# Moving the additions of weight blocks in DRAM out of the up-projection and into the part before it

## The chip, the cores and the metric

The kernel runs on one core of a Trainium2 chip. The metric is the device time of one execution in microseconds (us); the kernel before takes 1739.53 us as the median of 3 runs (1737.74 to 1740.78). The engines are called as in the profile: PE (matrix products), PEld (its weight loads), DVE (vector), ACT (scalar), POOL (GpSimd, which here only issues DMAs that add into their destination), and SP, whose queue issues nearly all other DMAs.

## The reference, cut to what matters

One decoder block on 256 tokens of width 2048, all in float32:

```
u    = rmsnorm(x)
proj = u @ w_in                     # columns of HGRN (q, f, i, gate), of attention (q, k, v), of two merge gates
ya   = hgrn2(...) @ w_proj_a        # gated linear recurrence, 16 heads of 128
yb   = dilated_attention(...) @ w_proj_b
mix  = sigmoid(gate_a) * ya + sigmoid(gate_b) * yb
h    = x + mix @ w_out
v    = rmsnorm(h)
hup  = v @ w_up                     # 2048 x 11264
hc   = causal_conv3(hup) + conv_b   # per channel
h    = h + (gelu(hc[:, :5632]) * hc[:, 5632:]) @ w_down
out  = rmsnorm(h)
```

## The kernel before, in words

**Units.** All weights lie in DRAM in the order of their use, as 300 units of 1 MB (128 partitions x 16 blocks of 128). Units 0 to 35 are the attention's columns of `w_in`, 36 to 99 those of HGRN, 100 to 131 the two gates, 132 to 151 `w_proj_b` and `w_proj_a`, 152 to 167 `w_out`, 168 to 299 the up-projection `w_up` in 11 blocks with pieces of `w_down` between them. `load(u)` has SP fetch a unit into one of three `raw` buffers (L303; L297 and L298 for the units described next). Each float32 weight is then cut into a high part, made by ACT (`hl`, L380), and the rest, made by DVE (L381), since a product is made from three PE passes: low input x high weight, high x high, high x low (L537 to L539 and L598 to L600). A pair of such parts stays in one of four `pair` buffers (six in the up-projection) until PE has read it. `begin_unit(u)` splits up to two units ahead of PE and loads three ahead.

**Two ways through w_up.** 88 units belong to `w_up`. 28 of them are mode "P" and have plain products. 60 are mode "S": seven products in place of eight, in the manner of Strassen and Winograd. An S unit needs sums of its four 512-column blocks of weights. Two of these sums, q1 and q2, are made in DRAM long before the unit is loaded; the others are made on DVE (L354, L355). `load` then fetches three blocks of the unit (L297), q1 as the fourth (L298, `raw<-q`) and q2 into a buffer of its own (L300, `q<-q`; two such buffers).

**The additions in DRAM.** The function `add_blocks` makes one turn. A turn starts q1 for the next S unit: SP copies a weight block to a DRAM tile (`q<-weights`, L266) and POOL adds another block to it by a DMA that adds (L267). The same turn also finishes the q2 of the S unit three turns earlier: SP copies its q1 (`q<-q`, L266, shown with a shape of 16x4096) and POOL adds a third block (L267). SP's copies stand behind the last weight load issued so far (`in_turn(loaded[-1])`). POOL's additions stand in POOL's queue in the order of the turns and each waits for its copy to land; SP's copy of q1 waits until the addition to q1 has landed. There are 60 S units and 63 turns, hence 120 copies and 120 additions of 256 KB.

**When a turn is taken.** `begin_unit(u)` makes turns until their number is `additions(u)`. In the kernel before that is 51 turns spread evenly from unit 44 to unit 166, and after that one turn every 8 units, up to unit 262. This means that the last 12 turns are made while `w_up` is worked on.

**The other work of POOL and ACT in w_up.** After a block of `w_up` its 512 columns are unfolded from seven PSUM banks (`up0v`, `up0c` and so on, with the block's number), transposed on PE (`ua3t`, `ub3t`, L1028), convolved (ACT writes the taps `ua3e`, `ub3e` at L1036, DVE adds them at L1038) and gated. Between blocks PE makes partial sums of `w_down` (`dn`). ACT copies each from PSUM to a buffer `dns` (L1078) and POOL adds it to `h` by a DMA (`h<-dns`, L1079). The buffers of `dns`, of the taps and of the unfolding come from one ring of five (`stage`), so one that waits for its DMA holds up ACT's next write into the ring.

**What sets the order.** Each engine has one queue and works in its order. The order is made by a scheduler from the program text, from priorities and from estimated durations, so that the place of an instruction can move when another one is moved. The diff touches only constants and the function `additions`.

Of the kernel before, what the change touches and what calls it, by code (L numbers as in the profile page):

```python
# [130 lines left out]
MODES = stream_spec()[1]  # L131

DRAM_SUMS = sorted(u for u, mode in MODES.items() if mode == "S")
ADD_FROM, ADD_TO, ADD_LATE = 44, 166, 8


def additions(u):
    n = len(DRAM_SUMS) + 3
    if u <= ADD_TO:
        return max(0, (u - ADD_FROM) * (n - 12) // (ADD_TO - ADD_FROM))  # L140
    return min(n, n - 12 + (u - ADD_TO) // ADD_LATE)

# [49 lines left out]
def hybrid_block(ctx, tc, x_p, x_t, weights, g1, gf, params, c_rope, c_mask0, c_mask1, c_level, out):  # L194
# [219 lines left out]
    def begin_unit(u):  # L414
        for v in range(u, u + LOOKAHEAD + 1):
            split(v)
        load(u + LOOKAHEAD + 1)
        pump(SIDE_US)
        while added[0] < additions(u):
            add_blocks()  # L420
            added[0] += 1
# [742 lines left out]
```

## Time and profile before

| what | value |
|---|---|
| time of the profiled execution | 1738.46 us |
| its span, first to last instruction | 1736.7 us |
| median of the runs | 1739.53 us |
| PE busy | 1713.5 us, 99% |
| DVE, ACT, POOL busy | 75%, 61%, 8% |
| mean granted PE clock | 0.998 |
| 16 DMA engines, mean moved | 240 GB/s |

The page divides the span into shares of busy time; a view of stretches gives the busy time of each engine between two times and the share of the DMA engines' time. A matmul's busy time overlaps that of the next (one starts some 0.23 us after the other and is shown with 0.39 us), so that a short wait of PE hardly shows in its busy time. The list of PE's waits and the number of matmuls in a stretch show it better. By the times at which the products of a stage start, the stages lie so: HGRN's columns to 619 us, the gates 619 to 805, `w_proj_b` and `w_proj_a` 805 to 917, `w_out` 917 to 1008, `w_up` and `w_down` from 1008 on.

### The profile page before, as it was taken

Reading aid. Unit: us, or ns where it says so; the run is one execution under the profiler, and the core shown is the slowest. Engines: PE = TensorE matmul, PEld = TensorE weight load, DVE = VectorE, ACT = ScalarE, POOL = GpSimd, SP = SyncE. Lnnn points to the kernel's source line nnn. Section 1 sums busy time; section 2 is a strip of 40 time slices with the busy share of each in tenths; the row PEclk is TensorE's granted clock in tenths of the full one; section 3 lists DMA queues with packets and bytes.
Section 4 is the critical chain, followed back from the end, with each engine's and each line's share of the span. In section 5 each row is a group of like instructions: output and inputs, shape, how many; then the busy total and the mean of one; then the engine's idle time right before and its main releaser. Section 6 shows DMA issues by size and latency. Waiting matters only on the chain. (4 is left out here: it accounts for less than half of the span.)

```text
span 1736.7 us, 22219 instructions
## 1 busy us (share of the span) xinstructions
PE 1713.5 (99%) x8292; PEld 1428.7 (82%) x8292; DVE 1301.3 (75%) x1559; ACT 1053.7 (61%) x1436; POOL 140.5 (8%) x181
## 2 busy tenths in 40 slices
PE   9999999999999999999999999999999999999998
PEld 8888888888888888888888887787777878888886
DVE  7765575776858675444656688999889889889886
ACT  6444465555455554544445568877776777887773
POOL 0000000011111011011111100110110110110000
PEclk9999999999999999999999999999999999999999
DMA  7765634778778787889998977887787788787672
GB/s 279 232 207 201 232 145 160 229 230 242 229 247 243 225 257 224 259 271 289 293 272 249 274 231 249 277 254 249 210 286 258 229 279 269 217 263 262 204 263 97
DMA packets 98684, 416.19 MB, mean 240 GB/s; under 512 B 11936, under 2 KB 12192, under 8 KB 67152
## 3 DMA queue, kind: packets, MB, share of 16 engines
q1 hardware_dynamic: 73344, 365.22, 58.5%
q0 software_dynamic: 23936, 46.15, 16.3%
q10 hardware_dynamic: 1296, 3.41, 0.5%
q8 instruction: 65, 1.06, 0.2%
q14 instruction: 43, 0.35, 0.1%
HBM read 400.05 MB, written 65.01 MB: 268 GB/s over the span
## 5 line engine op out<-in xcount | busy, mean ns | idle before, releaser
L380 ACT ACTIVATE hl<-raw 128x1024 fp32r<-128x1024 f32 (+1 forms) x480 | 500.9, 1055 | 502.1 <-PE egp L539 79.1
L381 DVE TENSOR_TENSOR hl<-raw,hl 128x1024 fp32r<-128x1024 f32 (+1 forms) x480 | 579.2, 1218 | 292.2 <-ACT hl L380 290.5
L267 POOL DMA_DIRECT2D q<-weights x120 | 99.7, 901 | 1113.3 <-DMA q<-q 821.3
L537 PE MATMUL dn<-hl,ff 128*128 128x512 f32 x320 | 126.7, 399 | 0.2 <-DVE up2c L621 0.2
L539 PE MATMUL dn<-hl,ff 128*128 128x512 f32 x320 | 125.0, 391 | 0.0
L538 PE MATMUL dn<-hl,ff 128*128 128x512 f32 x320 | 124.7, 390 | 0.0
L537 PE MATMUL egp<-hl,xu 128*128 128x512 f32 x256 | 100.5, 393 | 0.0
L539 PE MATMUL egp<-hl,xu 128*128 128x512 f32 x256 | 99.8, 390 | 0.0
L538 PE MATMUL egp<-hl,xu 128*128 128x512 f32 x256 | 99.7, 389 | 0.0
L328 DVE TENSOR_TENSOR se<-raw,se 128x1024 fp32r<-128x1024 f32 x60 | 73.2, 1221 | 16.6 <-ACT se L327 16.5
L327 ACT ACTIVATE sf<-raw 128x1024 fp32r<-128x1024 f32 x60 | 64.0, 1067 | 30.7 <-DVE raw L355 30.2
L328 DVE TENSOR_TENSOR sa<-raw,sa 128x1024 fp32r<-128x1024 f32 x60 | 73.2, 1220 | 9.8 <-ACT sa L327 9.8
L328 DVE TENSOR_TENSOR sf<-raw,sf 128x1024 fp32r<-128x1024 f32 x60 | 73.3, 1222 | 8.4 <-ACT sf L327 8.2
L327 ACT ACTIVATE se<-raw 128x1024 fp32r<-128x1024 f32 x60 | 63.9, 1066 | 25.1 <-PE up L600 12.6
L539 PEld LDWEIGHTS dn<-hl,ff 128*128 128x128 f32 x320 | 60.1, 188 | 13.1
L537 PEld LDWEIGHTS dn<-hl,ff 128*128 128x128 f32 x320 | 60.1, 188 | 12.7 <-DVE up2c L621 0.6
L538 PEld LDWEIGHTS dn<-hl,ff 128*128 128x128 f32 x320 | 60.2, 188 | 11.6
L327 ACT ACTIVATE sa<-raw 128x1024 fp32r<-128x1024 f32 x60 | 63.7, 1061 | 8.6 <-PE dn L539 4.9
L450 PE MATMUL ak<-xu,hl 128*128 128x512 f32 x192 | 67.1, 394 | 0.0
L539 PEld LDWEIGHTS egp<-hl,xu 128*128 128x128 f32 x256 | 48.1, 188 | 9.9
L538 PEld LDWEIGHTS egp<-hl,xu 128*128 128x128 f32 x256 | 48.1, 188 | 9.7
L537 PEld LDWEIGHTS egp<-hl,xu 128*128 128x128 f32 x256 | 48.1, 188 | 9.7
(585 smaller groups left out, 4417.6 us busy)
## 6 DMA issues: line engine op xcount, KB each, us to landing
raw<-weights SPq DMA_DIRECT2D x238, 1024.0 KB, 5.4
raw<-weights SPq DMA_DIRECT2D x60, 768.0 KB, 5.8
q<-weights POOLq DMA_DIRECT2D x120, 256.0 KB, 7.4
q<-q SPq DMA_DIRECT2D x120, 256.0 KB, 5.1
q<-weights SPq DMA_DIRECT2D x60, 256.0 KB, 6.3
raw<-q SPq DMA_DIRECT2D x60, 256.0 KB, 6.1
h<-dns POOLq DMA_DIRECT2D x36, 256.0 KB, 6.2
h<-x_t ACTq DMA_DIRECT2D x4, 512.0 KB, 6.6
```

The lines of the kernel that those rows point to most:

```text
L267: nc.gpsimd.dma_start(q, weights[u, :, i * 512 : (i + 1) * 512], accum_op=ALU.add)
L327: act.activation(hi, src, AF.Copy)
L328: vec.tensor_tensor(lo, src, hi.bitcast(F32), op=ALU.subtract)
L380: last[0] = act.activation(hi[:, q * w : (q + 1) * w], raw, AF.Copy)
L381: last[1] = vec.tensor_tensor(lo[:, q * w : (q + 1) * w], raw, hi[:, q * w : (q + 1) * w].bitcast(F32), op=ALU.subtract)
L450: pe.matmul(ps, hi, pair, start=(k == 0), stop=False, skip_group_check=True)
L537: pe.matmul(pst[m], xl, hi, start=(k == k0), stop=False)
L538: pe.matmul(pst[m], xh, hi, start=False, stop=False)
L539: pe.matmul(pst[m], xh, lo, start=False, stop=(k == k0 + nk - 1))
```

## The change

`additions` gets other constants. The turns now run from unit 40: 49 of them up to unit 132, at 0.533 per unit where it was 0.418, and the remaining 14 up to unit 166, at 0.412 per unit. From unit 168 on, where `w_up` begins, there are none. The number of turns, copies and additions is the same, and so are their sizes and everything that is computed.

```
-ADD_FROM, ADD_TO, ADD_LATE = 44, 166, 8
+ADD_FROM, ADD_THEN, ADD_TO, THEN_ADDS = 40, 132, 166, 14


 def additions(u):
     n = len(DRAM_SUMS) + 3
-    if u <= ADD_TO:
-        return max(0, (u - ADD_FROM) * (n - 12) // (ADD_TO - ADD_FROM))
-    return min(n, n - 12 + (u - ADD_TO) // ADD_LATE)
+    if u <= ADD_THEN:
+        return max(0, (u - ADD_FROM) * (n - THEN_ADDS) // (ADD_THEN - ADD_FROM))
+    return min(n, n - THEN_ADDS + (u - ADD_THEN) * THEN_ADDS // (ADD_TO - ADD_THEN))
```

PE and DVE work in the same order as before. What moves are instructions of SP and POOL, and one of ACT. In the rows below a name is the tile, its number (a unit's, or for `dns` and `dn` a block's with the quarter of the output) and a number of the tile's instance.

POOL in the first blocks of `w_up`, before: additions for later units stand between the additions of `w_down`'s partial sums.

```order
L267 DMA q2_269_7843<-weights 128x512
L267 DMA q1_273_8659<-weights 128x512
L1079 DMA h0_7267<-dns1_0_0_8772 128x512
L1079 DMA h0_7267<-dns1_0_1_8775 128x512
L1079 DMA h1_7269<-dns1_1_0_8837 128x512
L1079 DMA h1_7269<-dns1_1_1_8840 128x512
L267 DMA q2_270_7913<-weights 128x512
L267 DMA q1_274_9066<-weights 128x512
L1079 DMA h2_7271<-dns2_2_0_9251 128x512
L1079 DMA h2_7271<-dns2_2_1_9254 128x512
```

The same place after the change: the last addition for a weight block stands ahead of the first partial sum.

```order
L267 DMA q2_285_7587<-weights 128x512
L267 DMA q2_286_7657<-weights 128x512
L1079 DMA h0_7339<-dns1_0_0_8820 128x512
L1079 DMA h0_7339<-dns1_0_1_8823 128x512
L1079 DMA h1_7341<-dns1_1_0_8885 128x512
L1079 DMA h1_7341<-dns1_1_1_8888 128x512
L1079 DMA h2_7343<-dns2_2_0_9293 128x512
L1079 DMA h2_7343<-dns2_2_1_9296 128x512
```

All 21 additions that POOL made among or just ahead of these partial sums have moved to the time before `w_up`.

SP in the gates, before: two or three weight loads between two turns.

```order
L303 DMA raw116_5771<-weights 128x2048
L303 DMA raw117_5812<-weights 128x2048
L266 DMA q2_221_5482<-q1_221_5481 16x4096
L266 DMA q1_225_5814<-weights 128x512
L303 DMA raw118_5850<-weights 128x2048
L303 DMA raw119_5887<-weights 128x2048
L266 DMA q2_222_5580<-q1_222_5579 16x4096
L266 DMA q1_226_5889<-weights 128x512
L303 DMA raw120_5925<-weights 128x2048
L303 DMA raw121_5957<-weights 128x2048
L303 DMA raw122_5989<-weights 128x2048
L266 DMA q2_224_5681<-q1_224_5680 16x4096
```

The same units after the change: two, and at times only one.

```order
L303 DMA raw116_5831<-weights 128x2048
L303 DMA raw117_5872<-weights 128x2048
L266 DMA q2_238_5590<-q1_238_5589 16x4096
L266 DMA q1_246_5874<-weights 128x512
L303 DMA raw118_5910<-weights 128x2048
L303 DMA raw119_5947<-weights 128x2048
L266 DMA q2_244_5689<-q1_244_5688 16x4096
L266 DMA q1_248_5949<-weights 128x512
L303 DMA raw120_5985<-weights 128x2048
L266 DMA q2_245_5796<-q1_245_5795 16x4096
L266 DMA q1_249_5987<-weights 128x512
L303 DMA raw121_6023<-weights 128x2048
```

On ACT one row moves, after the second block of `w_up`. Before, the copy of the first partial sum stood ahead of two splits:

```order
L616 ACTIVATE up1c12_8724<-up1v_8719,rstd2_r_8015 128x512
L1078 ACTIVATE dns1_0_0_8772<-dn1_0_1_8735 128x512
L380 ACTIVATE hl186_0_8737<-raw186_8692 128x1024
L380 ACTIVATE hl186_1_8740<-raw186_8692 128x1024
L327 ACTIVATE sa187_8783<-raw187_8743 128x1024
```

Now it stands behind them:

```order
L616 ACTIVATE up1c12_8772<-up1v_8767,rstd2_r_8075 128x512
L380 ACTIVATE hl186_0_8785<-raw186_8740 128x1024
L380 ACTIVATE hl186_1_8788<-raw186_8740 128x1024
L1078 ACTIVATE dns1_0_0_8820<-dn1_0_1_8783 128x512
L327 ACTIVATE sa187_8831<-raw187_8791 128x1024
```

## The prediction

> **What bounds the kernel now.** I read the page's busy times first, then the stretches by stage, then PE's waits, and last the landings of DMAs and POOL's queue around the longest wait.
>
> ```profile
> PE 1713.5 (99%) x8292; PEld 1428.7 (82%) x8292; DVE 1301.3 (75%) x1559; ACT 1053.7 (61%) x1436; POOL 140.5 (8%) x181
> ```
>
> PE bounds the kernel: it is idle for 23 us of 1736.7. No change in transfers can give more than that. The view of stretches shows where (us of the stretch, then busy time and instructions of PE, PEld, DVE, ACT and POOL, clock, DMA share, GB/s):
>
> ```profile
> 297.00:619.00 322.00, 322.00 (x1740) 277.22 (x1739) 232.94 (x296) 168.72 (x206) 32.97 (x40) 1.00 0.77 235
> 619.00:805.00 186.00, 186.00 (x869) 155.30 (x868) 103.43 (x104) 90.69 (x100) 21.45 (x26) 1.00 0.85 257
> 805.00:917.00 112.00, 112.00 (x506) 92.32 (x505) 64.53 (x67) 46.95 (x48) 14.87 (x18) 1.00 0.94 284
> 917.00:1008.00 91.00, 91.00 (x417) 74.86 (x416) 58.88 (x79) 49.54 (x72) 11.51 (x14) 1.00 0.88 264
> 1050.00:1225.00 175.00, 169.99 (x766) 136.53 (x765) 160.04 (x186) 137.92 (x210) 15.42 (x18) 1.00 0.79 253
> 1225.00:1425.00 200.00, 192.43 (x860) 155.70 (x860) 173.96 (x199) 146.93 (x214) 17.36 (x20) 1.00 0.81 255
> 1425.00:1660.00 235.00, 235.00 (x1058) 193.06 (x1057) 215.19 (x247) 182.64 (x262) 15.51 (x19) 1.00 0.75 243
> ```
>
> From 297 to 1008 us PE is never idle, though turns run there all the time. From 1050 to 1425 it is idle for 5.01 + 7.57 = 12.58 us, and in the same kind of blocks from 1425 to 1660 not at all. The clock is 1.00 throughout. PE's waits from 1050 to 1425 name the causes (total us, times, longest):
>
> ```profile
> PE up L600 <- DVE sf L328: 4.6, 5, 1.6
> PE ub3t L1028 <- ACT ub3e L1036: 3.2, 1, 3.2
> PE up L598 <- DVE up0v L610: 1.5, 1, 1.5
> PE ua1t L1028 <- ACT ua1e L1036: 0.9, 1, 0.9
> PE up L598 <- ACT sf L327: 0.9, 1, 0.9
> PE ub5t L1028 <- ACT ub5e L1036: 0.6, 1, 0.6
> ```
>
> With three waits of 0.2 that are not shown the list comes to 12.3 us. So the question is which of them the turns cause, and what the turns cost where they go. The stretches of the additions alone (POOL busy, count) say how many are where:
>
> ```profile
> 1050.00:1225.00 175.00, 6.57 (x8) 1.00 0.79 253
> 1225.00:1425.00 200.00, 7.33 (x8) 1.00 0.81 255
> 1425.00:1660.00 235.00, 2.50 (x3) 1.00 0.75 243
> ```
>
> PE waits where 16 additions run, and does not where 3 do. That alone is only a coincidence in time; the longest wait shows a mechanism. The chain of waits around it (start, us, what), and ACT's row in the timeline:
>
> ```profile
> 1216.41 0.77 POOL q L267
> 1217.65 0.82 POOL q L267
> 1219.54 0.51 POOL h L1079
> 1220.10 14.66 DMA h<-dns
> 1231.12 0.47 ACT L1036 ACTIVATE ub3e<-ub3t,par 128x256 f32<-128x256 f32 x1 [3.60 <-DMA h<-dns]
> ```
>
> Two additions stand just ahead of a partial sum of `w_down` in POOL's queue. The partial sum then lands 14.66 us after its issue. Its `dns` buffer is of the ring of five, so ACT waits 3.60 us for a buffer for `ub3e`, and PE's transposes wait 3.2 us for ACT.
>
> **The change part by part.** *Taken out of w_up:* 21 additions with their 21 copies, 256 KB each (16 of the additions in the stretch that waits).
>
> 1. Waits behind `h<-dns`: `ub3t` 3.2 and `ub5t` 0.6. The minimum, median and maximum landing of `h<-dns` are, from 1050 to 1425 and then from 1425 to 1660:
>
> ```profile
> DMA to landing us min/median/max: 3.2/6.5/14.7
> DMA to landing us min/median/max: 3.2/6.2/9.9
> ```
>
> With no addition ahead I expect the later stretch's landings, where nobody waited. I take all 3.8 us.
>
> 2. Waits for the parts of S units (`sf`): 4.6 + 0.9 + 0.2 = 5.7 us. They go back to weight loads and q2 loads that land late. The first row below is the landing of q2 loads in this stretch, the others are from the chain of one such wait, in which a q2 load takes 11.77 us:
>
> ```profile
> DMA to landing us min/median/max: 2.5/3.4/12.2
> ...
> 1303.36 11.77 DMA q<-q
> 1315.21 0.64 ACT sg L327
> 1323.43 1.22 DVE sf L328
> ```
>
> The lower end is nothing (late because DVE is late), the upper end all 5.7. Against DVE as the cause: it is busy 160.04 + 173.96 = 334 of 375 us; in 375 - 11 us that would be 92%, and from 1425 to 1660 it was busy 215.19 of 235, also 92%, with PE never idle. So I take 85%: 4.8 us.
>
> 3. `ua1t`, and two of the waits of 0.2, 1.3 us in all: ACT came late to the taps of block 1. Its one moved row (the copy of `dns` now behind two splits) lets it use the time in which it waited for PE. I take half, 0.7. The wait for `up0v`, 1.5 us, follows a late weight load in block 0; I take a third, 0.5.
>
> The sum is 3.8 + 4.8 + 0.7 + 0.5 = 9.8 us. PE also loses its overlap at each wait. 766 + 860 matmuls at the later stretch's rate, 1058 in 235 us, would take 361.2 us in place of 375: 13.8 us where the waits say 12.3. So 9.8 x 13.8 / 12.3 = 11.0 us. The bounds are 4.3 (item 1 alone, so scaled) and 13.8 (every wait gone), to which the later stretch may add some 2 us when its own 3 additions go.
>
> *Put into HGRN and the gates.* A copy and an addition cost DMA time by the page's queues:
>
> ```profile
> q1 hardware_dynamic: 73344, 365.22, 58.5%
> q0 software_dynamic: 23936, 46.15, 16.3%
> q<-weights POOLq DMA_DIRECT2D x120, 256.0 KB, 7.4
> ```
>
> An addition of 0.262 MB is 0.262 / 46.15 x 16.3% of 1736.7 us = 1.61 us of all 16 engines; a copy is 0.262 / 365.22 x 58.5% = 0.73 us; together 2.34. The gates had 26 additions in 186 us at a share of 0.85. At 0.533 / 0.418 of the rate that is 33, so 7 more: 16.4 us, and a share of 0.94. That is the share that 805 to 917 us already has, with PE never idle. HGRN goes from 40 to 51 additions and from 0.77 to 0.85. After unit 132 the rate is 0.412 per unit where it was 0.418, so that the fullest stretch gets no fuller.
>
> What a fuller DMA does to weight loads is seen in their landings, from 700 to 805 us and then from 805 to 917:
>
> ```profile
> DMA to landing us min/median/max: 4.8/7.2/9.7
> DMA to landing us min/median/max: 4.8/7.1/9.2
> ```
>
> A load may take longer than that. There are three `raw` buffers, and a unit takes 186 / 32 = 5.8 us in the gates. After landing it needs two ACT splits and a DVE split:
>
> ```profile
> L381 DVE TENSOR_TENSOR hl<-raw,hl x124: 1200/1226/1227, 649.2 to 998.9; 128x1024 fp32r<-128x1024 f32 x124
> L380 ACT ACTIVATE hl<-raw x123: 1042/1061/1063, 650.8 to 997.8; 128x1024 fp32r<-128x1024 f32 x123
> ACT hl L380 <- PE egp L539: 73.2, 44, 2.6
> ```
>
> So a lasting landing above 3 x 5.8 - (2 x 1.06 + 1.23) = 14.0 us would hold PE up, and single ones of that length are covered by the pairs split ahead. ACT's splits wait for PE in the gates (73.2 us in 44 waits from 650 us on), not for the loads. I put 1 us on this part, with 0 as its lower end and the slow rival below as its upper one.
>
> *The new order on SP.* SP's copy of q1 waits until the addition three turns back has landed, and the next weight loads stand behind it. Three turns last 3 / 0.533 x 5.8 = 32.6 us. A copy lands after 11.5 us at most and an addition after 12.4 at most:
>
> ```profile
> DMA to landing us min/median/max: 4.9/6.2/11.5
> DMA to landing us min/median/max: 4.6/7.4/12.4
> ```
>
> With two POOL issues of 0.82 us that is 25.6 us, so no wait is added.
>
> **Result.** 1738.46 - 11.0 + 1.0 = 1728.5 us against the profiled execution. That execution lies 1.07 us under the median of the runs, so I say 1729 us.
>
> **The rivals.**
>
> - *The waits in w_up are ACT's and DVE's own* (chance 0.19). For it: ACT waits 19.2 us for DVE's sums from 1050 to 1425,
>
> ```profile
> ACT sf L327 <- DVE raw L355: 19.2, 15, 2.7
> ```
>
> DVE is busy 92% in what remains, and blocks 0 to 2 have other modes than those after 1425 us. Against it: the equal DVE share without waits later. Then only item 1 goes: 1739.5 - 4.3 = 1735 us.
> - *The DMA engines fill up under the gates* (0.09, slower). For it: 0.85 is a mean, and the end of the gates is fuller, with 8 additions in 50 us:
>
> ```profile
> 750.00:800.00 50.00, 50.00 (x223) 41.39 (x222) 23.11 (x19) 21.61 (x22) 6.55 (x8) 1.00 0.92 280
> ```
>
> If fuller rings lengthen the packets by a tenth, 0.94 becomes 1.03, and with the peaks some 8% of 186 us, 15 us, is lost: 1739.5 - 11 + 15 = 1743.5 us. It decides once weight loads take more than 14.0 us for many units on end. Against it: the stretch at 0.94 whose longest landing is 9.2.
> - *The memory itself binds in the gates, not the engines* (0.04). Each copy and addition is also written back to DRAM. The gates carry 257 GB/s moved and 52 x 0.262 MB / 186 us = 73 written back, 330 in all; with 66 such transfers they would carry 277 + 93 = 370. If 330 were the most, 12% of 186 us, 22 us, would be lost; but 805 to 917 us carries 284 + 36 x 0.262 / 112 = 368 without idle PE, so I take a quarter, 5.5 us: 1734 us. [...]
> - *The change does not do what it says* (0.02): the turns are late and still run under `w_up`. The order shows them ahead of it, so only a backlog in POOL's queue could do this: 1739.5.
>
> **How the numbers follow.** The likeliest case, 0.66, has its own range of 1723 to 1733 us. The range to hold 8 in 10 reaches down to 1722 (13.8 and 2 us gained, no cost in the gates, and a run that is 1.7 us fast, as the fastest of the three is) and up to 1737, which takes in the cases at 1734 and 1735. A change within 0.2%, 3.5 us, cannot be told from none. Faster: all of the likeliest case, 0.14 of the rival at 1735 and 0.03 of the one at 1734, 0.83. Same: 0.05, 0.03, 0.01 and 0.02, 0.11. Slower: 0.06.
>
> **What would show it.** Right: PE's idle time from 1050 to 1425 us falls from 12.6 us to under 4, `ub3t` and `ub5t` leave PE's waits, `h<-dns` never lands after more than 10 us, q2 loads neither, and the DMA share in `w_up` falls to some 0.72. In the gates the share is near 0.94, ACT waits for PE and not for loads, and PE has no idle time. Wrong: `sf` waits that stay with short landings (DVE's own lateness), `raw<-weights` among ACT's waits before 1008 us, or PE idle there; SP waiting for an addition in the gates would make the step on SP's order wrong.

## The result and the profile after

The changed kernel takes 1726.27 us (median of 4 runs, 1725.42 to 1727.29); beside it the kernel before took 1738.91 us (4 runs, 1737.74 to 1740.78). The ratio is 0.9931, with a 95% interval of 0.9919 to 0.9943, so it is faster by 0.7%. The profiled execution took 1727.29 us, with a span of 1725.5 us where it was 1736.7.

The view of stretches of the kernel after, in the columns of the prediction (us of the stretch, busy time and instructions of PE, PEld, DVE, ACT and POOL, clock, DMA share, GB/s):

```profile
297.00:619.00 322.00, 322.00 (x1740) 277.21 (x1739) 233.17 (x296) 167.74 (x206) 44.99 (x54) 1.00 0.89 260
619.00:805.00 186.00, 186.00 (x869) 155.31 (x868) 103.58 (x103) 91.55 (x100) 27.86 (x34) 1.00 0.93 271
805.00:917.00 112.00, 112.00 (x507) 92.35 (x506) 64.35 (x66) 47.06 (x49) 14.68 (x18) 1.00 0.94 293
1050.00:1225.00 175.00, 172.09 (x780) 139.58 (x779) 162.89 (x190) 140.81 (x215) 8.80 (x10) 1.00 0.72 236
1225.00:1425.00 200.00, 200.00 (x905) 164.55 (x904) 181.70 (x208) 157.39 (x231) 12.26 (x14) 1.00 0.72 237
```

PE's idle time from 1050 to 1425 us falls from 12.58 to 2.91 us, and PE starts 780 + 905 = 1685 matmuls there in place of 766 + 860 = 1626. Where the turns went, PE is idle nowhere, at DMA shares of 0.89, 0.93 and 0.94. PE's waits from 1008 us to the end (total us, times, longest):

```profile
PE up L598 <- DVE up0v L610: 1.6, 1, 1.6
PE up L598 <- ACT sf L327: 1.2, 1, 1.2
```

These two rows are all that is left. The minimum, median and maximum landing from 1050 to 1425 us, of `h<-dns` and then of the q2 loads:

```profile
DMA to landing us min/median/max: 3.2/5.0/8.0
DMA to landing us min/median/max: 2.5/2.7/7.6
```

Before, the maxima were 14.7 and 12.2.

**Where the 11.2 us of span came from.** The PE order is the same in both kernels, so that the same instruction can be looked up in both traces. Three groups of PE before (first and last start are the two numbers ahead of the semicolon): scores of the attention, the transposes of `h` under `w_out`, and the first transposes of `w_up`:

```profile
L704 PE MATMUL sc<-ak,aq x48: 270/326/382, 208.9 to 277.2; 128*128 128x128 f32 x24, 128*128 128x256 f32 x24
L999 PE MATMUL ht<-ident,h x32: 270/273/328, 940.7 to 1010.2; 128*128 128x128 f32 x32
L1028 PE MATMUL ua0t<-ident,up0c x8: 271/272/330, 1054.9 to 1066.4; 128*128 128x128 f32 x8
```

and after:

```profile
L704 PE MATMUL sc<-ak,aq x48: 270/326/382, 210.8 to 279.2; 128*128 128x128 f32 x24, 128*128 128x256 f32 x24
L999 PE MATMUL ht<-ident,h x32: 271/272/328, 942.7 to 1012.2; 128*128 128x128 f32 x32
L1028 PE MATMUL ua0t<-ident,up0c x8: 270/272/328, 1056.9 to 1068.4; 128*128 128x128 f32 x8
```

The changed kernel is 1.9 us late already at the scores, ahead of the first turn, and 2.0 us late under `w_out` and at the start of `w_up`. So all of HGRN, the gates and `w_out`, with 21 more additions and copies in them, cost 0.1 us at most. From there to the end it gains 2.0 + 11.2 = 13.2 us. The count of matmuls says the same: 59 more, at the later stretch's 235 us for 1058, are 13.1 us. All of it is won by 1425 us: the same matmul starts 2.0 us later than before at 1056 us, 11.1 us earlier at 1425 and 11.2 us earlier at the end.

### The profile page after: what moved, and what is told of

The parts are those of the page before. It is cut to its first block, busy times and chain, and to the rows that moved or that the text cites. A ratio compares the mean times of both kernels' runs of the same rounds, so it can differ in the third digit from the quotient of the medians.

```text
span 1725.5 us, 22221 instructions
## 1 busy us (share of the span) xinstructions
PE 1711.2 (99%) x8292; PEld 1429.8 (83%) x8292; DVE 1300.7 (75%) x1559; ACT 1054.4 (61%) x1436; POOL 140.2 (8%) x181
## 3 DMA queue, kind: packets, MB, share of 16 engines
HBM read 400.05 MB, written 65.01 MB: 270 GB/s over the span
## 5 line engine op out<-in xcount | busy, mean ns | idle before, releaser
L1079 POOL DMA_DIRECT2D h<-dns x36 | 31.6, 925 | 576.3 <-ACT dns L1078 572.4
L539 PEld LDWEIGHTS dn<-hl,ff 128*128 128x128 f32 x320 | 60.1, 188 | 13.0
L327 ACT ACTIVATE sa<-raw 128x1024 fp32r<-128x1024 f32 x60 | 63.6, 1059 | 11.4 <-PE dn L539 7.0
L537 PEld LDWEIGHTS dn<-hl,ff 128*128 128x128 f32 x320 | 60.1, 188 | 12.2 <-DVE up1c L617 0.2
L539 PEld LDWEIGHTS egp<-hl,xu 128*128 128x128 f32 x256 | 48.1, 188 | 10.0
L537 PEld LDWEIGHTS egp<-hl,xu 128*128 128x128 f32 x256 | 48.1, 188 | 9.7
```

Source lines behind the costliest of these rows:

```text
L327: act.activation(hi, src, AF.Copy)
L537: pe.matmul(pst[m], xl, hi, start=(k == k0), stop=False)
L539: pe.matmul(pst[m], xh, lo, start=False, stop=(k == k0 + nk - 1))
```

## The experiments

The theory was that of the prediction: late transfers in `w_up` make PE wait there, first of all additions that stand ahead of `h<-dns` in POOL's queue, and the early part hides them as long as weight loads land in under some 14 us. The rivals were that the waits belong to ACT and DVE, and that the early part is near a limit of its own. Each of the kernels below is built from the changed kernel.

**1. No turns at all.**

```
 def additions(u):
+    return 0
...
-            nc.sync.dma_start(r[:, 3 * 512 :], ready[u][0])
+            nc.sync.dma_start(r[:, 3 * 512 :], weights[u, :, 3 * 512 :])
...
-            nc.sync.dma_start(loaded_q[u], ready[u][1])
+            nc.sync.dma_start(loaded_q[u], weights[u, :, :512])
```

> No turns at all: the S units load plain weight blocks where q1 and q2 were, in the same sizes, so the products of w_up are not the reference's; PE, ACT and DVE have the order of the changed kernel. It measures what all 63 turns still cost where they are now. Theory (the gates and HGRN hide them, 1 us left): 1725.3 us, at most 1 us faster than the changed kernel, and PE's wait for up0v stays. Rival (the fuller DMA engines cost several us in the early part, and the gain under w_up was larger than seen): 1719 to 1722 us.

Measured: 1729.44 us (10 runs), ratio 0.9955 (0.9942 to 0.9968). The share in the gates falls to 0.51, and nothing is gained over the changed kernel. From the scores to the first transposes of `w_up` it takes 846.1 us (209.9 to 1056.0), as the changed kernel does with its turns (210.8 to 1056.9). So the turns cost nothing any more where they now lie. That the kernel without them is even slower, 1729 us where 1725.3 was expected, was a surprise. The row of the gates, PE's longest wait in `w_up` and the ACT row that it waits for (start, us, what, and in brackets the idle time before it):

```profile
619.00:805.00 186.00, 186.00 (x869) 155.40 (x868) 103.60 (x103) 91.43 (x101) 0.00 (x0) 1.00 0.51 181
...
PE ub2t L1028 <- ACT ua2e L1036: 2.5, 1, 2.5
...
1168.43 0.47 ACT L1036 ACTIVATE ua2e<-ua2t,par 128x256 f32<-128x256 f32 x1 [2.62 <-DMA h<-dns]
```

An `h<-dns` landed after up to 10.4 us with no addition for a weight block in the whole kernel. The wait of 2.5 us and the half clock after it (0.52 from 1172.7 to 1176.1 us; by the estimate of the last section 1.7 us) make 4.2 us; `w_up` began 0.9 us earlier, and the span is 3.2 us longer than that of the changed kernel, whose waits in `w_up` are otherwise the same within 0.3 us.

**2. and 3. The last ten turns back under w_up, at two sets of places.** The second run has them at the units at which a block ends and partial sums of `w_down` are added, the third has eight of them 4 units earlier, in the middle of blocks.

```
-ADD_FROM, ADD_THEN, ADD_TO, THEN_ADDS = 40, 132, 166, 14
+ADD_FROM, ADD_THEN, ADD_TO, THEN_ADDS, LATE_TURNS = 40, 132, 166, 14, [186, 196, 206, 218, 230, 242, 254, 266, 268, 270]
...
+    return min(made, n - len(LATE_TURNS)) + sum(t <= u for t in LATE_TURNS)
```

(third: `[182, 192, 202, 214, 226, 238, 250, 262, 268, 270]`)

> The changed kernel with its last 10 turns put back under w_up, one per block, where the partial sums of w_down are added (units 186, 196, 206, 218, 230, ...); PE, ACT and DVE keep the order of the changed kernel, its one moved ACT row too. Theory (partial sums wait in POOL's queue and rings behind additions, and loads land late): waits for taps (ub3t and the like) of 0.6 to 3 us come back in several blocks, h<-dns lands after over 10 us again, and the time is 1732 to 1738 us. Rival (the waits in w_up are ACT's and DVE's own, and the moved ACT row or chance made the gain): within 2 us of the changed kernel, 1725 to 1728 us.

> The same 10 turns under w_up, but in the middle of the eight w_up units of a block (units 182, 192, 202, 214, 226, ...), away from the partial sums; a few rows of ACT and DVE move by one or two places. Theory (two mechanisms, POOL's queue and late loads): no waits for taps behind h<-dns, only waits for sf parts, some 4 to 5 us, so 1730 to 1732 us, and clearly faster than with the turns at the partial sums. Rival (only the volume of DMA counts, not the place): the same time as with the turns at the partial sums, 1732 to 1738 us. Rival (ACT and DVE alone): 1726 us.

Measured: 1741.86 us at the block ends, ratio 1.0020 (1.0006 to 1.0034), and 1733.88 us in the middle, 0.9975 (0.9962 to 0.9987). Ten turns give back all of the gain or about half of it, by their place. PE's longest waits at the block ends:

```profile
PE ub1t L1028 <- ACT ub1e L1036: 3.2, 1, 3.2
PE ub2t L1028 <- ACT ua2e L1036: 2.4, 1, 2.4
PE ub3t L1028 <- ACT ub3e L1036: 2.3, 1, 2.3
PE up L600 <- DVE sf L328: 2.2, 4, 0.7
```

and in the middle (the wait for `up0v`, 1.6 us here and much the same in every kernel, is left out):

```profile
PE ub1t L1028 <- ACT ua1e L1036: 1.9, 1, 1.9
...
PE ua5t L1028 <- ACT ua5e L1036: 1.0, 1, 1.0
PE up L600 <- DVE sf L328: 0.9, 2, 0.6
```

The waits of the kernel before come back with the turns: the transposes (`ub1t` and so on) and the S units' parts (`sf`). They are not ACT's and DVE's own. At the block ends ten turns cost 15 us, more than expected (1732 to 1738 us): some 5 us of it is half clock (an estimate: the clock is 0.98 from 1050 to 1225 us and 0.99 from 1225 to 1425 us, which three stretches of 3.4 us at half clock give, 1.7 us each). In the middle only waits for `sf` parts were expected (1730 to 1732 us), and two waits for transposes came all the same: a place away from the partial sums makes the loss smaller but does not end it.

**4. and 5. More turns under the gates.** 0.75 and then 0.62 turns per unit from unit 100 to 166, in place of 0.533 and 0.412.

```
-ADD_FROM, ADD_THEN, ADD_TO, THEN_ADDS = 40, 132, 166, 14
+ADD_FROM, ADD_THEN, ADD_TO, THEN_ADDS = 40, 100, 166, 50
```

(0.62: `40, 100, 166, 41`)

> 13 turns up to unit 100 and the other 50 between 100 and 166, 0.76 per unit in the gates and after them; none under w_up. Theory (by 2.34 us of all engines for a copy with its addition, the share needed in the gates is 0.52 + 0.59 = 1.1, and 1.2 from 805 to 917 us): weight loads land after more than 14 us on end, PE waits for splits there, and the time is 1745 to 1785 us. Rival (packets are stretched by each other, so that the share near 1 still has room, and the shortest packets count): loads land after 10 to 13 us, PE hardly waits, 1726 to 1731 us.

> 22 turns up to unit 100 and 41 between 100 and 166, 0.62 per unit in place of 0.533 and 0.412; with 0.75 the time was 1757.8 us. Theory (it decides whether weight loads land after more than 14.0 us for many units on end, not what the share reads): in the gates the share is about 1.0, loads land after 9 to 12 us, PE is not idle; behind 805 us the share is about 1.0 and landings reach 10 to 14 us, which costs 0 to 5 us: 1726 to 1732 us. Rival (time is lost in proportion to the turns put there): 0.75 lost some 31 us against the changed kernel for 15 turns more behind unit 100 than the 0.53 and 0.41 would have; 0.62 loses about half of that, 1740 us or more.

Measured: 1757.83 us at 0.75, ratio 1.0115 (1.0091 to 1.0138), and 1728.65 us at 0.62, ratio 0.9936 (0.9922 to 0.9949). For 0.75, the stretches of the gates and of `w_proj_b` and `w_proj_a`, the landing of weight loads from 805 to 917 us, and ACT's longest wait from 620 to 1000 us:

```profile
619.00:805.00 186.00, 186.00 (x869) 155.28 (x867) 102.96 (x103) 90.32 (x99) 35.92 (x44) 1.00 1.01 300
805.00:917.00 112.00, 98.03 (x419) 78.66 (x418) 54.44 (x59) 38.39 (x42) 21.12 (x26) 0.95 1.04 307
...
DMA to landing us min/median/max: 10.7/14.6/17.3
...
ACT hl L380 <- DMA raw<-weights: 82.9, 23, 6.9
```

For 0.62 the stretch of `w_proj_b` and `w_proj_a` and the landing in it:

```profile
805.00:917.00 112.00, 110.91 (x499) 90.84 (x498) 63.63 (x66) 46.95 (x48) 20.93 (x26) 1.00 1.02 319
...
DMA to landing us min/median/max: 7.6/10.0/12.2
```

A share of 1.01 leaves PE busy all the time, at 1.02 it is idle for 1.1 us, and at 1.04 for 14 us. The share hardly tells these apart; the landings do, at a median of 10.0 against 14.6 us. With three `raw` buffers and 5.8 us per unit a load is on time up to some 14.0 us, as the prediction worked out, and the two runs lie on its two sides: no load over 12.2 us at 0.62, most over 14 at 0.75. Where between them the loss sets in no run shows. The time does not go up in proportion to the turns, which the rival of the fifth run said. At 0.75 the span is 31 us longer than that of the changed kernel: PE's waits from 619 to 1040 us come to 22.3 us, and the lower clock, 0.95 from 805 to 917 us and 0.98 from 917 to 1008 us, cost about 0.05 x 112 + 0.02 x 91 = 7.4 us more (an estimate).

**6. The changed kernel once more, and the turns spread evenly.**

```
-ADD_FROM, ADD_THEN, ADD_TO, THEN_ADDS = 40, 132, 166, 14
+ADD_FROM, ADD_THEN, ADD_TO, THEN_ADDS = 40, 166, 167, 0
```

> The changed kernel once more, unaltered, so that it stands on the same chip beside the runs below. It came out at 0.9931 of the kernel before; without any turns the kernel came out at 0.9955, in another session. If that order is real (the version without turns has a wait of its own in the third block, 2.5 us, followed by 3.4 us at half clock), this run shows 0.993 again, some 1726 us. If it was the session, it shows about 0.9955, 1730 us.

> All 63 turns spread evenly from unit 40 to unit 166 (0.5 per unit; the changed kernel has 0.533 to unit 132 and 0.412 behind it). PE, ACT, DVE and POOL work in the same order as in the changed kernel. Theory (the transfers under HGRN and the gates are hidden anyway, since PE is idle in neither): the share in the gates falls from 0.93 to about 0.9, from 805 to 917 us it rises from 0.94 to about 0.98, and the time stays within 0.2% of the changed kernel, 1724 to 1729 us. Rival (the stretch from 805 us on is at its limit at 0.94, so the lower rate behind unit 132 is needed): weight loads there land after more than 14 us, PE gets idle there, 1731 us or more.

Measured: 1726.0 us for the changed kernel, 0.9921 (0.9909 to 0.9934), and 1725.63 us evenly spread, 0.9923 (0.991 to 0.9935). The stretch that gets more turns:

```profile
805.00:917.00 112.00, 112.00 (x507) 92.34 (x506) 64.34 (x66) 47.19 (x49) 16.61 (x21) 1.00 0.98 302
```

The share rises to 0.98 and PE is not idle: the split at unit 132 makes no difference. The changed kernel comes out alike both times (0.9931 and 0.9921), ahead of the one without turns, which was run on one occasion only (0.9955; its interval from 0.9942 just touches that of the first).

**7. Late copies alone.** The second run's kernel without the 17 additions of its late turns.

```
-            nc.gpsimd.dma_start(q, weights[u, :, i * 512 : (i + 1) * 512], accum_op=ALU.add)
+            if added[0] < 53: nc.gpsimd.dma_start(q, weights[u, :, i * 512 : (i + 1) * 512], accum_op=ALU.add)
```

> The kernel with the last ten turns back under w_up at the block ends (1741.9 us), with POOL's 17 additions of those turns left out: SP's copies stay, every queue but POOL's has the same order, and the last S units get sums that lack a term or two. Theory (it is the additions ahead of the partial sums in POOL's queue that hurt, by the late h<-dns): h<-dns lands after 10 us at most, ub1t to ub4t leave PE's waits, and the time is 1726 to 1731 us. First rival (any transfer hurts, by its share of the 16 engines, 0.73 us of 2.34 for a copy): about a third of the loss of 15 us stays, 1731 to 1734 us. Second rival (the waits come from the split of a weight unit that falls on the block's end, whatever the transfers): 1738 us or more.

Measured: 1728.98 us, ratio 0.994 (0.9925 to 0.9956). Landings of `h<-dns` and of q2 from 1050 to 1425 us:

```profile
DMA to landing us min/median/max: 3.2/5.9/8.0
DMA to landing us min/median/max: 2.4/2.9/7.6
```

The additions do most of the harm: copies alone cost 3 us against the changed kernel (1726.0), where the whole turns cost some 15. But an addition is two things, a place in POOL's queue and time on the 16 DMA engines (1.61 us by the prediction's estimate). The next runs separate these.

**8. The additions' load without their place, and their place with less load.** The first puts two plain copies on SP's queue for each late addition left out, the second makes POOL's late additions plain copies in the same place. The second run's kernel stands beside them as a mark.

```
+        def instead(u, i):
+            return [nc.sync.dma_start(dram.tile([P, 512], F32, ...), weights[u, :, i * 512 : (i + 1) * 512]) for k in (0, 1)]
...
-                nc.sync.dma_start(q, src)
-            nc.gpsimd.dma_start(q, weights[u, :, i * 512 : (i + 1) * 512], accum_op=ALU.add)
+                nc.sync.dma_start(q, src), instead(u, i) if added[0] >= 53 else None
+            if added[0] < 53: nc.gpsimd.dma_start(q, weights[u, :, i * 512 : (i + 1) * 512], accum_op=ALU.add)
```

```
-            nc.gpsimd.dma_start(q, weights[u, :, i * 512 : (i + 1) * 512], accum_op=ALU.add)
+            nc.gpsimd.dma_start(q, weights[u, :, i * 512 : (i + 1) * 512], **({"accum_op": ALU.add} if added[0] < 53 else {}))
```

> The kernel with the last ten turns at the block ends once more, unaltered, as the mark on the same chip for the two runs below. It took 1741.9 us (ratio 1.0020) in its first session; 1.000 to 1.004 is expected again.

> As the run with the late copies alone (17 late additions left out, so that the last S units get sums that lack a term or two), but SP makes two plain copies of the same 256 KB to an unused DRAM tile for each addition left out. By the queues' rows two copies take 2 x 0.73 = 1.46 us of all 16 engines where an addition took 1.61, so the load on the DMA engines is that of the late additions and POOL's queue is that of the changed kernel. Theory (the additions hurt as queue mates of h<-dns on POOL): h<-dns lands after 10 us at most, 1727 to 1732 us. Rival (they hurt by the time that they take of the 16 engines, which the weight loads and h<-dns share): 1738 us or more, with the same transposes (ub1t to ub4t) among PE's waits. Between 1732 and 1738 both have a part.

> The run with the last ten turns at the block ends, but POOL's 17 late additions become plain copies (the same queue, place, size and waits; what lay in the tile is overwritten, so the last S units get a single block where a sum belongs). Theory (the place in POOL's queue counts): h<-dns still lands late behind them, over 10 us, and more than half of the loss of 15 us stays, 1735 to 1742 us. Rival (the time on the engines counts): a plain copy takes 0.73 us in place of 1.61, so under half stays, 1728 to 1734 us, and h<-dns lands after 10 us at most.

Measured, with the ratio and its interval:

| late under w_up, at the block ends | us | ratio | longest `h<-dns`, us |
|---|---|---|---|
| copies and additions (mark) | 1739.93 | 1.0006 (0.9994 to 1.0017) | 14.8 |
| copies, and two plain copies on SP per addition | 1736.91 | 0.9997 (0.9987 to 1.0007) | 12.3 |
| copies, and plain copies on POOL | 1729.55 | 0.9953 (0.9938 to 0.9968) | 10.8 |
| copies alone (run 7) | 1728.98 | 0.994 (0.9925 to 0.9956) | 8.0 |

The first theory, the place in POOL's queue, most likely holds for the smaller part only: with POOL's queue as empty as in the changed kernel, the load alone brings back 1736.91 - 1728.98 = 7.9 of 11.0 us (by the ratios, since run 7 was measured apart from the other three, 9.9 of 11.5). With the load on SP, around the second block's end, first POOL, then SP's queue, and ACT:

```profile
1160.15 0.87 POOL L1079 DMA_DIRECT2D h<-dns  x1 [46.24 <-ACT dns L1078]
...
1162.09 0.33 SPq L303 DMA_DIRECT2D raw<-weights  x1
1162.48 0.48 SPq L266 DMA_DIRECT2D q<-q  x1
1163.01 1.34 SPq L257 DMA_DIRECT2D x<-weights  x2
1164.39 0.66 SPq L266 DMA_DIRECT2D q<-weights  x1
1165.09 1.43 SPq L257 DMA_DIRECT2D x<-weights  x2
...
1172.20 0.47 ACT L1036 ACTIVATE ua2e<-ua2t,par 128x256 f32<-128x256 f32 x1 [2.75 <-DMA h<-dns]
...
DMA to landing us min/median/max: 3.2/8.1/12.3
```

One `h<-dns` after the other goes out on a queue that holds nothing else, and ACT still waits 2.75 us for one of them: a weight load and six block copies were issued from another queue in the same 5 us. So a queue of their own did not keep these transfers clear of the others: with the load on SP the longest `h<-dns` landed after 12.3 us, with the copies alone after 8.0. The plain copies on POOL take 0.84 us of the 16 engines each and the additions 1.55 (from the shares of POOL's queue, 15.7%, 16.3% and, without either, 14.9%, over 17; the shares are rounded, so about 0.1 us either way). With that half of the load in the same place, little of the loss comes back: one wait like that of run 1, 2.5 us with its half clock. Two things stay open. The other 3 us of the mark are within the noise, since the intervals of the first two rows overlap; if they are real, no run divides them between POOL's queue and what an addition does in the engines. And the load on SP was larger than the additions': the share of SP's queue, 60.1% with the 34 substitutes and 57.7% (mark) or 58.6% (run 7) without, gives these some 1.0 to 1.2 us each, where 0.73 was meant, so that two of them took 1.9 to 2.4 us for an addition's 1.55. Part of the 7.9 us may be that surplus. That transfers from another queue make `h<-dns` late is shown (12.3 against 8.0 us); that they outweigh the place in POOL's queue is likely, not shown.

## Why the prediction was right

Forecast were 1729 us and a range of 1722 to 1737; measured are 1726.27 and, a second time, 1726.0. In part that was luck, since misses cancelled: `w_up` gained 13.2 us where 11.0 was forecast and the early part cost 0.1 where 1.0 was, but 2.0 us were lost ahead of the first turn, which no term had. By the steps of the prediction:

- **Item 1, `ub3t` and `ub5t`, 3.8 us: all taken, as said.** The cause was put down to the two additions ahead in POOL's queue. By run 8 that is most likely the smaller part: more (there 7.9 of 11.0 us) comes from the time that the turn's transfers take on the DMA engines just when `h<-dns` goes out. The number did not depend on which it was, since the change moves the transfers and their place together. The mark and run 3 show that a turn's place among the blocks counts.
- **Item 2, the `sf` waits, 85% of 5.7 us.** By the same list 4.5 us went, against 4.8. The ratio was right, but the list of PE's waits is too short a measure. The list of the waits of PEld (PE's weight loads, which by these rows wait for the parts `sf` and `sg` too) had from 1050 to 1425 us before:

```profile
PEld up L600 <- DVE sf L328: 7.2, 7, 2.0
PEld up L598 <- ACT sf L327: 1.6, 2, 1.3
PEld up L600 <- DVE sg L328: 0.8, 2, 0.6
```

and after:

```profile
PEld up L598 <- ACT sf L327: 1.7, 1, 1.7
PEld up L600 <- DVE sf L328: 1.2, 3, 0.4
```

- **Item 3.** `ua1t` and the small waits went whole (1.3 us, where 0.7 was taken). The wait for `up0v`, of which a third was to go, stays at 1.6 us, and it is there in every kernel run here, the one without turns too (1.6 us): the turns do not cause it.
- **The mis-sized term is the factor for lost overlap.** The rows of waits that went sum to 12.3 - 2.8 = 9.5 us, where 9.8 was forecast, but 13.2 us were gained: a factor of 1.39, not 13.8 / 12.3 = 1.12. The yardstick was the rate of the stretch behind 1425 us, taken as the best that these blocks could do with no wait at all; the changed kernel comes to 1685 / 375 = 4.49 matmuls per us, against 1058 / 235 = 4.50 there, with 2.8 us of waits left. These blocks can run faster than that stretch. What PE's list leaves out shows in the starts of the same matmuls in both traces. A wait is shown from the end of the matmul ahead, 0.39 us after its start, while without a wait the next one starts after 0.23; so by estimate (0.39 - 0.23) a wait costs some 0.16 us more than is shown, and one under 0.16 us is not shown at all. `ub3t` starts 3.60 us after the matmul ahead of it in the kernel before and 0.24 us after it in the changed one: 3.4 us for a wait shown as 3.2. From 1056 to 1425 us, 8 matmuls that follow over 0.5 us closer make up 10.1 us of the 13.1, and 13 that follow 0.1 to 0.5 us closer another 2.4. All rows of PEld's waits together go from 23.6 to 8.3 us, 15.3 less, so that the gain lies between the two lists.
- **The early part, +1.0 us with 0 as its lower end.** It cost 0.1 us at most from 209 to 1012 us. The share in the gates was 0.93 (0.94 forecast), in HGRN 0.89 (0.85 forecast, with 51 additions where 54 came). ACT waited there for PE, with one wait of 1.8 us for a weight load: that is one of the prediction's signs of being wrong, but PE was not idle for it. The late start of 2.0 us lies ahead of all turns and was in no term; in the second profile of the changed kernel it was 0.9 us.
- **SP's order** added no wait, as worked out.
- **The rivals.** "ACT's and DVE's own" falls with runs 2 and 3. "The DMA engines fill up" has its mechanism, and runs 4 and 5 lie on the two sides of the 14.0 us estimated for it, but at this density the kernel is clear of it: the longest load from 805 to 917 us landed after 11.4 us. "The memory binds": in the gates the changed kernel moves 271 GB/s and writes back an estimated 68 x 0.262 MB / 186 us = 96 (over the whole span the page has 65.01 MB written, and 240 transfers of 0.262 MB are 62.9), 367 in all without idle PE, and at 0.62 it is by the same estimate 319 + 52 x 0.262 / 112 = 441 from 805 to 917 us, with PE idle for 1.1 us. So no limit of the memory showed up to there.

## What to carry to other kernels

A transfer that is off the critical path can still set the end where it falls beside a short one that an engine waits for (with the load on SP's queue, ACT waited 2.75 us for an `h<-dns`); its queue is not all that counts, and by these runs most likely less than how many microseconds of all DMA engines are asked for in that moment (7.9 of 11.0 us came back with the load alone), so such work belongs under stages whose buffers look ahead further than the transfers take to land (here an estimated 14.0 us against 11.4 us at most). How far such a stage can be filled is read from the landings against the buffers (here a median of 10.0 us went with a time under 3 us longer, one of 14.6 us with over 30), not from the DMA share, which read 1.01 with PE still busy. When waits are priced, the list of PEld's waits stands beside that of PE's, and where two traces have the same order, the starts of the same instructions say what a wait really cost: here, with 13.1 us, it lay between the two lists (9.5 and 15.3 us).

## What had not been expected of the hardware

**Half clock behind some short waits.** After some waits PE was granted half its clock for 3.4 us. Stretches of the run with plain copies on POOL, ahead of such a dip, in it and behind it:

```profile
1166.00:1172.70 6.70, 4.17 (x21) 3.24 (x20) 4.55 (x7) 4.64 (x9) 0.97 (x2) 1.00 1.05 318
1172.70:1176.10 3.40, 3.40 (x10) 2.61 (x9) 3.40 (x4) 2.46 (x4) 0.00 (x0) 0.50 0.78 221
1176.10:1179.50 3.40, 3.40 (x16) 2.79 (x16) 1.57 (x3) 3.40 (x8) 0.00 (x0) 1.00 1.01 381
```

and of the kernel before, ahead of the end of its longest wait and behind it:

```profile
1230.00:1233.80 3.80, 0.59 (x4) 0.17 (x2) 0.77 (x1) 2.60 (x5) 0.00 (x0) 1.00 0.56 185
1233.80:1237.20 3.40, 3.40 (x17) 2.92 (x18) 2.52 (x4) 2.35 (x4) 0.90 (x2) 1.00 0.02 5
```

In the dip 10 matmuls start in 3.4 us, behind it 16. By the clock the dip cost half of 3.4 us, 1.7 us, and by these counts 3.4 x (1 - 10 / 16) = 1.3 us (estimates), on top of a wait of 2.5 us. In the kernel before, the wait of 3.2 us was not followed by one, and with the load on SP the clock is 1.00 from 1175.7 to 1179.1 us, behind a wait of 2.6 us.

A dip, with 1.7 us by the clock, takes 0.01 off the clock of a stretch of 175 to 235 us, so that the clock of the stretches from 1050 to 1225, 1225 to 1425 and 1425 to 1660 us gives the number of dips (an estimate, since the clock is rounded):

| profile | clock of the three | dips | PE's waits of 1.8 us or more from 1008 to 1720 us |
|---|---|---|---|
| kernel before | 1.00, 1.00, 1.00 | 0 | 3.2 |
| changed kernel, both times; runs 5 and 7 | 1.00, 1.00, 1.00 | 0 | none (longest 1.6, 1.5, 1.6 and 1.7) |
| run 1 | 0.99, 1.00, 1.00 | 1 | 2.5 |
| run 2 | 0.98, 0.99, 1.00 | 3 | 3.2, 2.4, 2.3 |
| the mark of run 8 | 0.98, 0.99, 1.00 | 3 | 2.7, 2.4, 1.8 |
| run 3 | 0.99, 1.00, 1.00 | 1 | 1.9 |
| turns evenly spread (run 6) | 0.99, 1.00, 1.00 | 1 | 1.8 |
| load on SP (run 8) | 0.99, 1.00, 1.00 | 1 | 2.6, 2.1, 1.9, 1.8 |
| plain copies on POOL (run 8) | 0.99, 1.00, 1.00 | 1 | 2.5 |

So, run 4 aside, 11 dips stand against 15 such waits. The length of a wait alone does not decide: a profile with one wait of 3.2 us has no dip, and one whose longest wait is 1.8 us has one. What decides it no run here shows.

**A small loss ahead of the turns.** In all profiles of kernels built from the changed one, that without turns among them, the attention's products for `aq` take a median of 398 to 399 ns where they took 391 before, and the scores start 0.8 to 0.9 us later against these products than before. PE's order is the same, and no addition runs there. The cause is open.
